# Feed-forward networks: x normed first from the third unit pair on, its two parts side by side in one moving operand of 512 columns

## The chip, the cores and the metric

The kernel runs on one core of one Trainium2 chip. The metric is the device time of one execution in microseconds (us), as the median of several runs.

## The reference, cut to what matters

One sequence of 256 tokens with 1024 channels goes through two small transformer stacks. Three of their stages are dense feed-forward networks, and only those are touched: one of the first stack (`ffn`), and two with a causal convolution of width 3 over the tokens in the second (`ffa`, `ffb`).

```
D_MODEL = 1024; SEQ = 256; D_FF = D_FF_2 = 2816

def rms_norm(x, g):
    y = x * rsqrt(mean(x * x, axis=-1) + EPS)
    return y * g

def swiglu(h, w_gate, w_up, w_down):                       # ffn
    return (silu(h @ w_gate) * (h @ w_up)) @ w_down

def conv_glu_ffn(h, w_in, conv_w, conv_b, w_out):          # ffa, ffb
    u = h @ w_in
    c = causal_conv(u, conv_w, width=3) + conv_b           # each channel by itself
    a, g = c[..., :D_FF_2], c[..., D_FF_2:]
    return (a * silu(g)) @ w_out

x = x + swiglu(rms_norm(x, ffn_norm[0]), ...)
h = h + conv_glu_ffn(rms_norm_2(h, norm_ffn[i]), ...)      # i = 0, 1
```

Around them stand a convolution stage, two attention stages, a mixture of experts and a pooling stage. All values are float32.

## The kernel before, in words

**Layout.** x stays in SBUF as `self.x`, channels on the 128 partitions: eight tiles of 128 channels, 256 tokens each. All weights come from DRAM as units of 128x2048 float32 (1 MB), in one fixed order, by the class `Stream`. TensorE multiplies in float32r. To keep float32 accuracy each operand is split into a high part (rounded to float32r) and a low part (the rest), and each product is made of three: high weights by high x, high weights by low x, low weights by high x (`mm3`, L468).

**The stream.** `load` (L304) sends SP's DMA for a unit into one of six `raw` buffers. `h` (L350) makes the high part `wh` on ScalarE (ACT, L359), `l` (L362) the low part `wl` on VectorE (DVE, L370) by subtraction. There are four `wh` and three `wl` buffers. `adv` (L380) goes to the next unit. So `h` works up to four units ahead of TensorE (PE) and `l` up to three. The order of the instructions on each engine is that of the code: nothing is reordered by a scheduler, and each engine takes its instructions in order.

**A feed-forward network (`ffn`, L918).** The 2816 inner channels are worked in 11 pairs of units, p = 0 to 10: the gate unit and the up unit of 256 inner channels. The order of the units is gate 0, up 0, gate 1, up 1, then gate p, up p, down p-2 for p = 2 to 10, and down 9 and down 10 at the end.

- Before it, `residual` (L627) adds the last stage to x, makes x times the norm's gain in two parts (`xh`, `xl`, L607 and L613) and sums the squares. The factor 1/rms of each token is not yet known then.
- `unit_B` (L473) multiplies one unit: for each of its two halves m of 128 inner channels and each of 8 channel tiles k three matmuls of 256 columns, 48 in all, into one PSUM bank with the two halves side by side.
- During pair 0 the sums of squares go through PE, and DVE makes 1/rms (L544 to L576). `bcast` brings it to all partitions as `rb` (L591, ACT).
- Since `xh` and `xl` lack 1/rms, the product is multiplied by `rb` as it leaves PSUM: one DVE operation of 512 columns, in `scaled` (L925, without convolution) or `convolved` (L936, with it, into the padded tile `cu`).
- `convolved` then makes tap 0 on ACT (L939) and taps 1 and 2 on DVE (L947, two operations of 256 columns each).
- `gate_out` adds Silu on ACT (L955). DVE multiplies up by gate (L973), ACT makes the high part of it (L975), DVE the low part (L982). These two halves are the moving operand of the down unit two pairs later (`unit_down`, L491, 48 matmuls of 256 columns).
- Calls of `st.h()` and `st.l()` stand between these steps, so the parts of later units are made on ACT and DVE between the steps of the current pair.

The PSUM banks of the gate and up units have the tag "g", of which there are four; the down units' sums have four more. Big SBUF tiles (`self.big`, 128x2048) come from a pool of six in turn.

Of the kernel before, what the change touches and what calls it, by code (L numbers as in the profile page):

```python
# [6 lines left out]
F32 = mybir.dt.float32  # L7
F32R = mybir.dt.float32r
I32 = mybir.dt.int32
AF = mybir.ActivationFunctionType  # L10
ALU = mybir.AluOpType
# [3 lines left out]
P = 128  # L15
S = 256
D = 1024
NT = D // P
# [57 lines left out]
def unit_plan():  # L76
# [8 lines left out]
    def ffn(ph, gate, up, g0, u0, down):  # L85
# [5 lines left out]
        for p in (NP_FF - 2, NP_FF - 1):  # L91
            u.append((ph, "row", down, 256 * p))

    ffn("ffn", "gate", "up", 0, 0, "down")
    for p in range(4):
        u.append(("att", "col", "w_kvf", 256 * p))
# [7 lines left out]
    for e in range(NE):  # L104
# [8 lines left out]
        u.append(("moe", "row", ("mdown", e), 2560))  # L113
    u.append(("pool", "pool", "pool", 0))
    ffn("ffa", "in0", "in0", FF, 0, "out0")
    u.append(("at2", "col", "qkv", 1024))
    for what in ATT2:
# [4 lines left out]
        elif what[0] == "o" and what[-1] != "+":  # L122
            u.append(("at2", "rowq", "o2", int(what[1])))
    ffn("ffb", "in1", "in1", FF, 0, "out1")
    return u

# [279 lines left out]
class Builder:  # L406
# [66 lines left out]
    def unit_B(self, tag, xs):  # L473
# [11 lines left out]
                    self.mm3(o, H[:, w], L[:, w], xs[0][:, a], xs[1][:, a], k == 0, k == NT - 1)  # L485
        return ps

    def acc_new(self):
        return [self.bank("acc") for _ in range(4)]

# [424 lines left out]
        return acc  # L915


    def ffn(self, xs, total, conv=None):  # L918
        nc, st = self.nc, self.st
        acc = None  # L920
        rb = None

        def scaled(ps, name):
            t = self.wk.tile([P, 512], F32, name=name)
            nc.vector.tensor_tensor(out=self.v2(t), in0=self.v2(ps), in1=self.rb2(rb), op=ALU.mult)  # L925
            st.h()
            st.l()
            return t

        def convolved(ps, tile0, name):  # L930

            W = S + 2
            up = self.wk.tile([P, 2 * W], F32, name="cu", tag="w1", bufs=4)
            u3 = up.rearrange("p (a w) -> p a w", a=2)
            nc.gpsimd.memset(u3[:, :, 0:2], 0.0)
            nc.vector.tensor_tensor(out=u3[:, :, 2:W], in0=self.v2(ps), in1=self.rb2(rb), op=ALU.mult)  # L936
            o = self.wk.tile([P, 512], F32, name=name)
            for m in range(2):
                nc.scalar.activation(out=o[:, m * S:(m + 1) * S], in_=up[:, m * W:m * W + S], func=AF.Identity,  # L939
                                     scale=self.c(f"fw{conv}", 3 * (tile0 + m), 1),  # L940
                                     bias=self.c(f"fb{conv}", tile0 + m, 1))
            st.h()
            st.l()
            for k in (1, 2):
                for m in range(2):
                    q = o[:, m * S:(m + 1) * S]
                    nc.vector.scalar_tensor_tensor(q, up[:, m * W + k:m * W + k + S],  # L947
                                                   self.c(f"fw{conv}", 3 * (tile0 + m) + k, 1), q,
                                                   op0=ALU.mult, op1=ALU.add)
            return o  # L950

        def gate_out(p, gps):
            t = scaled(gps, "gs") if conv is None else convolved(gps, 22 + 2 * p, "gs")
            sg = self.wk.tile([P, 512], F32, name="sg")
            nc.scalar.activation(out=sg, in_=t, func=AF.Silu)  # L955
            return sg

        pend = []
        for p in range(NP_FF):
            gps = self.unit_B("g", xs)  # L960
            st.adv()
            if p:
                sg = gate_out(p, gps)
                ups = self.unit_B("g", xs)
            else:
                r = self.stats(total)
                st.l()
                ups = self.unit_B("g", xs)
                rb = self.bcast(r)
                sg = gate_out(p, gps)  # L970
            st.adv()
            u = scaled(ups, "us") if conv is None else convolved(ups, 2 * p, "us")
            nc.vector.tensor_tensor(out=u, in0=u, in1=sg, op=ALU.mult)  # L973
            ah, al = self.parts()
            nc.scalar.activation(out=ah, in_=u, func=AF.Copy)  # L975
            if len(pend) == 2:
                if acc is None:
                    acc = self.acc_new()
                self.unit_down(acc, [pend.pop(0)], p == 2, False)
                st.adv()  # L980
                st.h()
            nc.vector.tensor_tensor(out=al, in0=u, in1=ah.bitcast(F32), op=ALU.subtract)  # L982
            st.l()
            pend.append((ah, al))
        self.unit_down(acc, pend, False, True)
        st.adv()
        st.adv()
        return acc
# [920 lines left out]
    def run(self):  # L1909
        st, ph = self.st, self.phases  # L1910
        st.h()
        st.l()
        st.h()
        upd = None
        if "conv" in ph:
            upd = self.added(self.conv(), "cbo")
        if "ffn" in ph:
            upd = self.added(self.ffn(*self.residual(upd, "gf0")))
        if "att" in ph:
            upd = self.added(self.att1(upd))  # L1920
        if "moe" in ph:
            upd = self.moe(upd)
        if "pool" in ph:
            upd = self.pool(upd)
        if "ffa" in ph:
            upd = self.added(self.ffn(*self.residual(upd, "hf0"), 0))
        if "at2" in ph:
            upd = self.added(self.att2(upd))
        if "ffb" in ph:
            upd = self.added(self.ffn(*self.residual(upd, "hf1"), 1))  # L1930
            self.final(upd)
            return
        if upd is not None:
            for b in range(4):
                upd(b)
        self.nc.sync.dma_start(out=self.A["out"], in_=self.x)
# [17 lines left out]
```

## Time and profile before

| | us |
|---|---|
| median of 3 runs | 1762.65 (1759.74 to 1765.97) |
| the profiled execution, its own time | 1759.57 |
| its span | 1757.8 |
| PE busy | 1705.6 (97% of the span) |
| PE weight loads busy | 1536.7 (87%) |
| DVE busy | 1394.4 (79%) |
| ACT busy | 1095.3 (62%) |

The page of a profile shows the busy time of each engine, the span in 40 slices, the DMA queues, the chain of work that ended last, and the costliest groups of instructions. Behind it stand other views of the same execution: the chain of waits in order of time, the timeline of one engine, and tables by stretches of time. Matmuls are pipelined, so the duration in a matmul's row is longer than the time from one start to the next. The pace of PE is read from the starts. The three networks lie at about 130 to 330 us (`ffn`), 1282 to 1473 us (`ffa`) and 1558 to 1749 us (`ffb`).

### The profile page before, as it was taken

What the parts mean: (1) busy time and instruction counts of PE and PEld (TensorE: products, weight loads), DVE (VectorE), ACT (ScalarE), POOL (GpSimd) and SP (SyncE); (2) the same over time, 40 slices, a digit from 0 to 9 for tenths busy, and PEclk for the clock granted to TensorE, in tenths of its full rate; (3) what the DMA queues carried; (4) which work ended last, traced back from release to release, by engine and by line L of the source; (5) the groups of instructions that cost most, each with busy time, mean ns of one, the idle gap of its engine ahead of it and who ended that gap; (6) DMA issues with size and microseconds to landing.
All of it is one profiled execution on the core that took longest, in us unless ns stands there. A gap on an engine that the chain in (4) does not pass through costs nothing. (4 is left out here: it accounts for less than half of the span.)

```text
span 1757.8 us, 26713 instructions
## 1 busy us (share of the span) xinstructions
PE 1705.6 (97%) x10780; PEld 1536.7 (87%) x10781; DVE 1394.4 (79%) x1649; ACT 1095.3 (62%) x1209; POOL 69.6 (4%) x114
## 2 busy tenths in 40 slices
PE   7979999999999999999999999999899999899998
PEld 6879999988888888888888888888789999899998
DVE  6976555765688988998998988988797777978766
ACT  4954443654587777777777777777555545756543
POOL 2800000010000000000000000000000000000000
PEclk9989999999999999999999999999999999999999
DMA  7235554443499799999999899999545554335440
GB/s 285 96 120 207 178 192 172 165 169 120 163 363 366 285 359 345 377 337 365 346 354 376 337 354 347 367 355 370 190 167 199 184 191 156 141 121 195 189 144 25
DMA packets 60560, 429.35 MB, mean 244 GB/s; under 512 B 6912, under 2 KB 6928, under 8 KB 9232
## 3 DMA queue, kind: packets, MB, share of 16 engines
q1 hardware_dynamic: 59760, 425.48, 64.8%
q0 software_dynamic: 672, 2.11, 0.4%
q8 instruction: 86, 1.41, 0.3%
q14 instruction: 42, 0.34, 0.1%
HBM read 426.50 MB, written 1.06 MB: 243 GB/s over the span
## 5 line engine op out<-in xcount | busy, mean ns | idle before, releaser
L370 DVE TENSOR_TENSOR wl<-raw,wh 128x2048 fp32r<-128x2048 f32 x384 | 870.2, 2286 | 41.0 <-PE ps_acc L466 20.4
L359 ACT ACTIVATE wh<-raw 128x2048 fp32r<-128x2048 f32 x384 | 734.0, 1915 | 243.3 <-PE ps_g L466 115.9
L466 PE MATMUL ps_g<-xh,wh 128*128 128x256 f32 x1136 | 322.7, 284 | 3.9 <-ACT xh L607 3.9
L466 PE MATMUL ps_g<-xl,wh 128*128 128x256 f32 x1136 | 323.4, 285 | 3.1 <-DVE xl L613 3.1
L466 PE MATMUL ps_g<-xh,wl 128*128 128x256 f32 x1136 | 321.9, 283 | 0.0
L466 PE MATMUL ps_g<-wh,xgh 128*128 128x512 f32 x704 | 276.5, 393 | 0.0
L466 PE MATMUL ps_g<-wh,xgl 128*128 128x512 f32 x704 | 274.3, 390 | 0.0
L466 PE MATMUL ps_g<-wl,xgh 128*128 128x512 f32 x704 | 274.2, 390 | 0.0
L466 PE MATMUL ps_acc<-parts,wh 128*128 128x256 f32 x1312 | 239.0, 284 | 0.7 <-DVE parts L511 0.5
L466 PE MATMUL ps_acc<-wh,parts 128*128 128x512 f32 x704 | 226.6, 392 | 4.2 <-ACT parts L510 4.2
L466 PEld LDWEIGHTS ps_g<-xl,wh 128*128 128x128 f32 x1136 | 218.4, 192 | 5.0 <-DVE xl L613 5.0
L466 PEld LDWEIGHTS ps_g<-xh,wh 128*128 128x128 f32 x1136 | 218.5, 192 | 4.2 <-ACT xh L607 4.1
L466 PEld LDWEIGHTS ps_g<-xh,wl 128*128 128x128 f32 x1136 | 218.5, 192 | 0.0
L466 PEld LDWEIGHTS ps_acc<-parts,wh 128*128 128x128 f32 x1312 | 204.7, 192 | 2.1 <-issue 0.9
L466 PE MATMUL ps_acc<-parts,wl 128*128 128x256 f32 x656 | 185.6, 283 | 0.0
L466 PEld LDWEIGHTS ps_acc<-wh,parts 128*128 128x128 f32 x704 | 131.4, 188 | 36.4 <-ACT parts L510 6.4
L466 PEld LDWEIGHTS ps_g<-wh,xgl 128*128 128x128 f32 x704 | 132.1, 188 | 28.1
L466 PEld LDWEIGHTS ps_g<-wh,xgh 128*128 128x128 f32 x704 | 132.3, 188 | 26.3
L466 PEld LDWEIGHTS ps_g<-wl,xgh 128*128 128x128 f32 x704 | 132.3, 188 | 26.2
L466 PE MATMUL ps_acc<-wl,parts 128*128 128x512 f32 x352 | 137.2, 390 | 0.7 <-DVE wl L370 0.7
L466 PEld LDWEIGHTS ps_acc<-parts,wl 128*128 128x128 f32 x656 | 125.9, 192 | 0.0
L511 DVE TENSOR_TENSOR parts<-ps_acc,parts 128x512 fp32r<-128x512 f32 (+1 forms) x48 | 31.0, 647 | 68.7 <-ACT parts L510 68.7
(309 smaller groups left out, 1970.1 us busy)
## 6 DMA issues: line engine op xcount, KB each, us to landing
raw<-ws SPq DMA_DIRECT2D x390, 1024.0 KB, 6.2
ahead<-ws SPq DMA_DIRECT2D x10, 1024.0 KB, 7.1
raw<-ws SPq DMA_DIRECT2D x4, 512.0 KB, 8.6
ck<-cdram POOLq DMA_DIRECT2D x8, 256.0 KB, 5.6
x<-xt SPq DMA_DIRECT2D x2, 512.0 KB, 4.2
out<-o SPq DMA_DIRECT2D x4, 256.0 KB, 2.3
cb<-cb SPq DMA_DIRECT2D x1, 617.5 KB, 15.5
raw<-band SPq DMA_DIRECT2D x1, 527.0 KB, 6.0
```

Source lines behind the costliest of these rows:

```text
L359: self.nc.scalar.activation(out=self.hi[i], in_=self.raw[i], func=AF.Copy)
L370: self.nc.vector.tensor_tensor(out=t, in0=raw, in1=self.hi[i].bitcast(F32), op=ALU.subtract)
L466: self.nc.tensor.matmul(out, lhsT, rhs, start=start, stop=stop, skip_group_check=True)
L511: self.nc.vector.tensor_tensor(out=l, in0=src, in1=h.bitcast(F32), op=ALU.subtract)
```

## The change

From pair 2 on, the gate and up units take a new moving operand, and their results leave PSUM in another way.

- Two new big tiles `ya` and `yb` hold x, normed with its gain and with `rb`, in two parts: for each channel tile k the 256 columns of the high part and, right beside them, the 256 of the low part. `normed(b)` makes two channel tiles of it: two DVE operations of 256 columns (x times gain times `rb`, into `xn`), one ACT copy of 512 columns (high part), one DVE subtraction of 512 columns (low part). `normed(0)` and `normed(1)` (into `ya`, k = 0 to 3) stand at the end of pair 0, `normed(2)` and `normed(3)` (into `yb`, k = 4 to 7) in pair 1, ahead of the step that takes the up product out of PSUM.
- `unit_W` multiplies a unit: for each half m and tile k one matmul of high weights by 512 columns (both parts), and one of low weights by the 256 columns of the high part. That is 32 matmuls in place of 48. Each half m has a PSUM bank of its own, in which the first 256 columns are a part of the sum and the other 256 the rest.
- `summed` takes a unit out of PSUM: for each half an ACT copy of the second 256 columns into SBUF and a DVE addition of the first 256. It takes the place of one DVE multiplication by `rb` of 512 columns.

Pairs 0 and 1 stay with `unit_B`, `xh`, `xl` and the multiplication by `rb`.

```diff
+    def unit_W(self, tag, ys):
+        H, L = self.st.cur()
+        pss = []
+        for m in range(2):
+            ps = self.bank(tag)
+            for k in range(NT):
+                w = slice(k * 256 + m * P, k * 256 + m * P + P)
+                y, o = ys[k // 4], (k % 4) * 512
+                self.mm(ps, H[:, w], y[:, o:o + 512], k == 0, False)
+                self.mm(ps[:, 0:S], L[:, w], y[:, o:o + S], False, k == NT - 1)
+            pss.append(ps)
+        return pss
...
-    def ffn(self, xs, total, conv=None):
+    def ffn(self, xs, total, gain, conv=None):
...
+        ys = [self.big(F32R, "ya"), self.big(F32R, "yb")]
+
+        def normed(b):
+            t = self.wk.tile([P, 512], F32, name="xn", tag="w1", bufs=4)
+            for m in range(2):
+                j = 2 * b + m
+                nc.vector.scalar_tensor_tensor(t[:, m * S:(m + 1) * S], self.x[:, j, :], self.c(gain, j, 1), rb,
+                                               op0=ALU.mult, op1=ALU.mult)
+            y = ys[b // 2][:, 1024 * (b % 2):1024 * (b % 2) + 1024].rearrange("p (a c s) -> p a c s", a=2, c=2)
+            nc.scalar.activation(out=y[:, :, 0, :], in_=self.v2(t), func=AF.Copy)
+            nc.vector.tensor_tensor(out=y[:, :, 1, :], in0=self.v2(t), in1=y[:, :, 0, :].bitcast(F32),
+                                    op=ALU.subtract)
+
+        def products(p):
+            return self.unit_W("g", ys) if p > 1 else self.unit_B("g", xs)
+
+        def summed(dst, ps, p):
+            if p < 2:
+                nc.vector.tensor_tensor(out=dst, in0=self.v2(ps), in1=self.rb2(rb), op=ALU.mult)
+                return
+            for m in range(2):
+                nc.scalar.activation(out=dst[:, m, :], in_=ps[m][:, S:2 * S], func=AF.Copy)
+                nc.vector.tensor_tensor(out=dst[:, m, :], in0=ps[m][:, 0:S], in1=dst[:, m, :], op=ALU.add)
...
-            nc.vector.tensor_tensor(out=u3[:, :, 2:W], in0=self.v2(ps), in1=self.rb2(rb), op=ALU.mult)
+            summed(u3[:, :, 2:W], ps, p)
...
             st.adv()
-            u = scaled(ups, "us") if conv is None else convolved(ups, 2 * p, "us")
+            if p == 1:
+                for b in (2, 3):
+                    normed(b)
+            u = scaled(ups, p, "us") if conv is None else convolved(ups, p, 2 * p, "us")
...
             nc.vector.tensor_tensor(out=al, in0=u, in1=ah.bitcast(F32), op=ALU.subtract)
+            if p == 0:
+                for b in (0, 1):
+                    normed(b)
             st.l()
```

The change moves instructions at these places. The rows are in the order in which the engine takes them.

DVE in `ffa`, from the end of pair 0 to the end of pair 1, before (`cu<-ps_g` is a product leaving PSUM, `wl` the low part of a later unit, `gs` and `us` the taps of gate and up):

```order
L982 TENSOR_TENSOR parts<-us,parts 128x512
L936 TENSOR_TENSOR cu<-ps_g,rb 128x2x256
L370 TENSOR_TENSOR wl<-raw,wh 128x2048
L947 SCALAR_TENSOR_TENSOR gs<-cu,cb,gs 128x256 x4
L936 TENSOR_TENSOR cu<-ps_g,rb 128x2x256
L370 TENSOR_TENSOR wl<-raw,wh 128x2048
L947 SCALAR_TENSOR_TENSOR us<-cu,cb,us 128x256 x4
```

The same stretch with the change:

```order
L1027 TENSOR_TENSOR parts<-us,parts 128x512
L946 SCALAR_TENSOR_TENSOR xn<-x,ca,rb 128x256 x2
L950 TENSOR_TENSOR ya<-xn,ya 128x2x256
L946 SCALAR_TENSOR_TENSOR xn<-x,ca,rb 128x256 x2
L950 TENSOR_TENSOR ya<-xn,ya 128x2x256
L959 TENSOR_TENSOR cu<-ps_g,rb 128x2x256
L370 TENSOR_TENSOR wl<-raw,wh 128x2048
L989 SCALAR_TENSOR_TENSOR gs<-cu,cb,gs 128x256 x4
L946 SCALAR_TENSOR_TENSOR xn<-x,ca,rb 128x256 x2
L950 TENSOR_TENSOR yb<-xn,yb 128x2x256
L946 SCALAR_TENSOR_TENSOR xn<-x,ca,rb 128x256 x2
L950 TENSOR_TENSOR yb<-xn,yb 128x2x256
```

The twelve new DVE operations of a network stand in two blocks, one ahead of gate 1's way out of PSUM, one behind gate 1's taps and ahead of up 1's way out.

PE at the start of gate 2 in the change (a wait for DVE is written behind the instruction that has it):

```order
L466 MATMUL ps_g<-xh,wl 128x256
L466 MATMUL ps_g<-ya,wh 128x512 [waits DVE_49]
L466 MATMUL ps_g<-ya,wl 128x256
L466 MATMUL ps_g<-ya,wh 128x512
L466 MATMUL ps_g<-ya,wl 128x256
L466 MATMUL ps_g<-ya,wh 128x512 [waits DVE_49]
L466 MATMUL ps_g<-ya,wl 128x256
L466 MATMUL ps_g<-ya,wh 128x512
L466 MATMUL ps_g<-ya,wl 128x256
L466 MATMUL ps_g<-yb,wh 128x512 [waits DVE_49]
L466 MATMUL ps_g<-yb,wl 128x256
```

Where every tile k had three matmuls of 256 columns there are now one of 512 and one of 256, and PE waits for DVE ahead of every second k, once for each `normed(b)`.

## Rows read from the trace of the kernel before

**Rows 1.** The page: busy time of each engine, share of the span, instructions.

```profile
PE 1705.6 (97%) x10780; PEld 1536.7 (87%) x10781; DVE 1394.4 (79%) x1649; ACT 1095.3 (62%) x1209; POOL 69.6 (4%) x114
```

**Rows 2.** Chain of waits, `ffa` and `ffb`: start us, us, what.

```profile
1282.92 33.45 PE ps_g L466 x277
1316.37 5.76 PE ps_acc L466 x48
1322.13 11.52 PE ps_g L466 x96
...
1443.09 11.54 PE ps_g L466 x96
...
1461.30 10.96 PE ps_acc L466 x89
...
1592.38 5.76 PE ps_acc L466 x48
```

**Rows 3.** Timeline of PE, mixture of experts: start us, us, engine, line, op, tiles.

```profile
704.34 0.39 PE L466 MATMUL ps_g<-wl,xgh 128*128 128x512 f32 x1
704.57 0.39 PE L466 MATMUL ps_g<-wh,xgl 128*128 128x512 f32 x1
...
706.84 0.39 PE L466 MATMUL ps_acc<-wh,parts 128*128 128x512 f32 x1
```

**Rows 4.** Timeline of DVE, `ffa`, pairs 0 and 1.

```profile
1301.42 0.69 DVE L973 TENSOR_TENSOR us<-us,sg 128x512 f32<-128x512 f32 x1
1302.81 0.69 DVE L982 TENSOR_TENSOR parts<-us,parts 128x512 fp32r<-128x512 f32 x1 [0.70 <-ACT parts L975]
1303.42 0.68 DVE L936 TENSOR_TENSOR cu<-ps_g,rb 128x512 f32<-128x512 f32 x1
1304.03 2.28 DVE L370 TENSOR_TENSOR wl<-raw,wh 128x2048 fp32r<-128x2048 f32 x1
1306.22 1.67 DVE L947 SCALAR_TENSOR_TENSOR gs<-cu,cb,gs 128x256 f32<-128x256 f32 x4
1307.81 0.69 DVE L936 TENSOR_TENSOR cu<-ps_g,rb 128x512 f32<-128x512 f32 x1
```

**Rows 5.** Timeline of ACT, `ffa`, pair 0.

```profile
1293.37 0.39 ACT L591 ACTIVATE rb<-ps_g 128x256 f32<-128x256 f32 x1 [7.60 <-PE ps_g L466]
...
1302.15 0.63 ACT L975 ACTIVATE parts<-us 128x512 fp32r<-128x512 f32 x1 [1.36 <-DVE us L973]
```

**Rows 6.** Timeline of DVE, `ffa`: operations of 256 columns, from SBUF and from PSUM.

```profile
1278.05 0.86 DVE L1791 SCALAR_TENSOR_TENSOR x<-ps_acc,cb,x 128x256 f32<-128x256 f32 x2
...
1282.40 0.87 DVE L613 SCALAR_TENSOR_TENSOR xl<-x,ca,xh 128x256 fp32r<-128x256 f32 x2
1283.19 1.14 DVE L535 TENSOR_TENSOR sq<-sq 128x512 f32<-128x512 f32 x2
```

**Rows 7.** Timeline of DVE, `ffb`, gate 1 leaves PSUM.

```profile
1579.82 0.68 DVE L936 TENSOR_TENSOR cu<-ps_g,rb 128x512 f32<-128x512 f32 x1
```

**Rows 8.** Timeline of DVE, `ffn`, pair 1.

```profile
148.00 0.68 DVE L925 TENSOR_TENSOR gs<-ps_g,rb 128x512 f32<-128x512 f32 x1
148.59 2.28 DVE L370 TENSOR_TENSOR wl<-raw,wh 128x2048 fp32r<-128x2048 f32 x1
153.03 0.69 DVE L925 TENSOR_TENSOR us<-ps_g,rb 128x512 f32<-128x512 f32 x1 [2.15 <-PE ps_g L466]
```

**Rows 9.** Stretches of 3 us: length, PE busy, granted clock, DMA share, GB/s.

```profile
462.00:465.00 3.00, 2.07 (x10) 0.50 0.09 36
465.00:468.00 3.00, 2.86 (x13) 0.50 0.00 0
...
1249.00:1252.00 3.00, 0.87 (x4) 1.00 0.06 19
1252.00:1255.00 3.00, 1.18 (x5) 0.80 0.15 22
1255.00:1258.00 3.00, 3.00 (x19) 0.63 0.80 330
1258.00:1261.00 3.00, 3.00 (x28) 1.00 0.01 3
```

**Rows 10.** Waits of DVE, 1283 to 1475 us: us in total, times, longest us.

```profile
DVE cu L936 <- PE ps_g L466: 29.8, 16, 2.7
```

More of the change, by code (lines that the diff above doesn't have):

```diff
@@ L921, in ffn, with scaled @@
         rb = None
-        def scaled(ps, name):
+        ys = [self.big(F32R, "ya"), self.big(F32R, "yb")]
[18 more added lines that the diff above has]
+                nc.vector.tensor_tensor(out=dst[:, m, :], in0=ps[m][:, 0:S], in1=dst[:, m, :], op=ALU.add)
+        def scaled(ps, p, name):
             t = self.wk.tile([P, 512], F32, name=name)
-            nc.vector.tensor_tensor(out=self.v2(t), in0=self.v2(ps), in1=self.rb2(rb), op=ALU.mult)
+            summed(self.v2(t), ps, p)
             st.h()
@@ L928, in scaled, with convolved @@
             return t
-        def convolved(ps, tile0, name):
+        def convolved(ps, p, tile0, name):
             W = S + 2
@@ L952, in gate_out @@
         def gate_out(p, gps):
-            t = scaled(gps, "gs") if conv is None else convolved(gps, 22 + 2 * p, "gs")
+            t = scaled(gps, p, "gs") if conv is None else convolved(gps, p, 22 + 2 * p, "gs")
             sg = self.wk.tile([P, 512], F32, name="sg")
@@ L959, in ffn @@
         for p in range(NP_FF):
-            gps = self.unit_B("g", xs)
+            gps = products(p)
             st.adv()
@@ L963, in ffn @@
                 sg = gate_out(p, gps)
-                ups = self.unit_B("g", xs)
+                ups = products(p)
             else:
@@ L967, in ffn @@
                 st.l()
-                ups = self.unit_B("g", xs)
+                ups = products(p)
                 rb = self.bcast(r)
@@ L1917, in run @@
         if "ffn" in ph:
-            upd = self.added(self.ffn(*self.residual(upd, "gf0")))
+            upd = self.added(self.ffn(*self.residual(upd, "gf0"), "gf0"))
         if "att" in ph:
@@ L1925, in run @@
         if "ffa" in ph:
-            upd = self.added(self.ffn(*self.residual(upd, "hf0"), 0))
+            upd = self.added(self.ffn(*self.residual(upd, "hf0"), "hf0", 0))
         if "at2" in ph:
@@ L1929, in run @@
         if "ffb" in ph:
-            upd = self.added(self.ffn(*self.residual(upd, "hf1"), 1))
+            upd = self.added(self.ffn(*self.residual(upd, "hf1"), "hf1", 1))
             self.final(upd)
```

## Prediction

> **What bounds the kernel now.** I read the page first: PE is busy for 97% of the span [rows 1], so time is won or lost where PE's stream is dense or broken. Then the chain of waits in the networks: in `ffa` it is PE alone from 1282.92 us to the end of the last up unit at 1454.63, in blocks of 5.76 us for 48 matmuls [rows 2]. That is 120 ns for each matmul of 256 columns, with no gap. A unit that is faster on PE therefore shortens a network one for one, and a stall of PE lengthens it one for one: nothing behind it has slack to give back. Last, the timelines of DVE and ACT around pairs 0 to 2, since the new operand is made there.
>
> The reader should see one thing in rows 4. Pair 1's gate product leaves PSUM on DVE at 1303.42, without a wait in its row, and the up product at 1307.81, again without one. Counted back from the down unit at 1316.37, up 2 runs from 1310.61, gate 2 from 1304.85, up 1 from 1299.09 [rows 2]. So gate 1 was done at 1299.09 and waited 4.3 us for DVE, and up 1 was done at 1304.85 and waited 3.0 us. DVE is behind in pairs 0 and 1, and later it waits for PE (29.8 us in 16 waits in `ffa`, [rows 10]). It costs nothing today, because only later units need what it makes. The change makes gate 2 need it at once.
>
> **The gain on PE.** In the mixture of experts eleven matmuls of 512 columns start between 704.34 and 706.84: 227 ns each [rows 3]. One of 512 and one of 256 columns take 227 + 120 = 347 ns, three of 256 take 360: 13 ns less. A unit has 16 such places: 0.21 us less (5.55 in place of 5.76). Nine pairs by two units by three networks are 54 units: 11.3 us. The rows' pace fits 13.3 ns for each matmul beside its columns (120 = 106.7 + 13.3 at 2.4 GHz, 227 = 213.3 + 13.3), and the change saves one such piece in three.
>
> The Trainium skill (TensorE: Matmul & The Clock Gate, section Back-to-back issue gap) gives a warm gap of N/2.4 + 2.5 ns. By that rule a place saves 2.5 ns and all 54 units 2.2 us. The rows of this kernel decide for 13.3.
>
> **The stall at gate 2.** A block `normed(b)` on DVE is two operations of 256 columns, a round trip to ACT, and one of 512 columns. The pair of L613 lasts 0.87 [rows 6]. From the end of DVE's L973 (1302.11) to the start of ACT's copy (1302.15) are 0.04, the copy takes 0.63, and DVE starts 0.03 later [rows 4, 5]. The subtraction lasts 0.69, and the next operation starts 0.61 after it. So a block takes 0.87 + 0.04 + 0.63 + 0.03 + 0.61 = 2.18 us of DVE's queue, and its part is ready 2.26 after its start. DVE takes its instructions in order, so it idles during the round trip. I take the rows as they are; without the round trip a block is 0.79 + 0.61 = 1.4, and with every operation 0.1 longer it is 2.6.
>
> In `ffa` the first block starts where L936 stood, at 1303.42. The parts for k = 0, 1 are ready at 1305.68, those for k = 2, 3 at 1307.86. Then come the old steps from L936 to the next L936 (1303.42 to 1307.81, 4.39 us, [rows 4]), and the third block starts at 1303.42 + 4.36 + 4.39 = 1312.17: k = 4, 5 ready at 1314.43, k = 6, 7 at 1316.61. PE could start gate 2 at 1304.85; two tiles k take it 0.69. It runs in four pieces at 1305.68, 1307.86, 1314.43 and 1316.61, then half m = 1 without a wait (2.78): the end is 1316.61 + 0.69 + 2.78 = 1320.08, where it was 1310.61. **9.5 us lost**, gate 2's own gain included.
>
> `ffb` has the same steps: the block starts at 1579.82 [rows 7], gate 2 could start at 1592.38 - 11.52 = 1580.86 [rows 2]. The last part is ready at 1593.01, gate 2 ends at 1596.48 in place of 1586.62: **9.9 lost**.
>
> `ffn` has no taps on DVE. The blocks start at 148.00 and up 1 ends at 153.00 [rows 8], so `ya` (152.44) is in time. Then gate 1's L925 (0.59) and a `wl` (2.20): the third block starts at 155.15, k = 4, 5 are ready at 157.41, k = 6, 7 at 159.59. PE reaches k = 4 at 154.39 and stands. Gate 2 ends at 163.06 in place of 158.76: **4.3 lost**.
>
> Together 23.7. The other 17 units of each network give back 51 x 0.21 = 10.7.
>
> **The clock.** The granted clock falls after PE has stood still. Between 1249 and 1255 PE was busy for 2.05 of 6 us, and the clock then read 0.80 and 0.63 and was full again at 1258 [rows 9]. With a lower level of half speed that is 0.4 x 3 + 0.74 x 3 = 3.4 us at half. In `ffa` and `ffb` PE would work 2.8 of some 12 us. I take one such 3.4 us each, in which PE would have done 1.7 us of work more: 3.4. At least nothing; at most twice that in each network (462 to 468 has 6 us at half, [rows 9]) and 1.7 in `ffn`: 8.5.
>
> **What hides, and the rest.** The way out of PSUM changes from one DVE operation (0.61 to the next) to two ACT copies (0.39 each by L591, [rows 5]) and two DVE additions (0.43 each by L1791, [rows 6]). A pair gains 4 x 0.43 - 2 x 0.61 = 0.5 us of DVE work and loses 0.4 of length; DVE's waits for PE, up to 2.7 us at one place, cover both [rows 10]. If that cover were gone, `wl` would be late next, and PE with it. At the end of `ffa` and `ffb` it is not hidden: after the last up unit (1454.63) PE waits for that product's parts, and the chain goes on at 1461.30 [rows 2], 6.67 later, while one down unit covers 5.76 and a few matmuls of the next the rest. There one half's copy and addition (0.39 + 0.07 + 0.43) take the place of 0.61: 0.3 each, 0.6 in all. ACT's copies queue behind its Silu and `wh`; ACT is busy 62% [rows 1], and `wh` is made a unit earlier than `wl`. A product now takes two of the four banks "g": gate 3 needs gate 2's, which are out a whole up and down unit earlier; up 2's second half needs up 1's, out by 1317.2, before gate 2's end. The two big tiles shift which buffer each later tile gets; their former owners are done by then, and SP's load of attention constants at the end of `ffa` falls on `xh`, last read in up 1. No DMA is added or moved past another; POOL's two small fills per pair stay where they are. All this at nothing.
>
> **Sum.** 23.7 - 10.7 + 3.4 + 0.6 = +17.0 us, against the profiled execution's own 1759.57: 1776.6. The median of the runs is 3.1 above that execution, which would make 1779.6. I say 1778. Bounds: with blocks of 1.4 the last parts come at 1313.5, 1589.9 and 156.5, the losses are 6.4, 6.8 and 1.2, and without clock and tail the sum is +4; with blocks of 2.6 the losses are 11.2, 11.6 and 6.0, and with 8.5 for the clock and 0.6 for the tail it is +27.
>
> **The rivals.**
> - *Forecast (0.62):* the stall outweighs the gain, one short fall of the clock.
> - *The clock stays low (0.17):* 8.5 in place of 3.4, so 1783. For it: gate 2 has four pieces with gaps between them. Against: after 1258 it was back at once.
> - *PE gets hardly faster (0.04):* if the 512 columns went at 237 to 240 ns beside a 256, 9 to 11.3 us of the gain are gone: 1787 to 1789. For it: no row before shows the two lengths in turn. Against: both lengths keep their pace over long runs [rows 2, 3]. The rule of the Trainium skill (same page and section) would give 1787; the rows so far don't bear it out.
> - *No stall, faster (0.08):* the parts are in time, and the kernel has its 11.3 less: 1750. It decides at k = 6 of gate 2: `normed(3)` must be ready by about 1307 in `ffa`. That holds if DVE isn't late there. For it: DVE has long waits in all later pairs. Against: rows 4 show none in pair 1, and DVE's order is fixed.
> - *They cancel (0.09):* blocks without the round trip and no fall of the clock: +4, 1764 to 1767. For it: ACT might find the copy's input earlier. Against: the same round trip stands in every pair, with 0.70 us of idle DVE [rows 4].
>
> **How the numbers follow.** About 0.3% (5.3 us) is what a measurement of this kernel can tell from no change. Slower: 0.62 + 0.17 + 0.04 = 0.83. Same 0.09, faster 0.08. The range leaves out the faster case, most of the cancelling one, and sums over +27: 1767 to 1790.
>
> **What would show it.** In the new trace, PE's waits in gate 2 for DVE's L950 should come to some 9.7 us in `ffa`, 10 in `ffb` and 4.5 in `ffn`; blocks from down 0 on should read 11.1 us for 64 matmuls of gate and up, in place of 11.52 for 96; the granted clock should dip once at each of the two long stalls. No waits for L950 would make the forecast wrong, a pair of gate and up at 11.5 or a stall at every pair would make it too small.

## The result, and the profile after

The change made the kernel slower: 1787.66 us (median of four executions, 1784.01 to 1796.61) against 1762.52 for the kernel before, measured beside it; ratio 1.0138 [1.0110, 1.0167]. The profiled execution took 1785.67 us, its span is 1783.9 (before 1757.8, so 26.1 more).

The rest of the kernel, whose code is the same in every run, varies from one execution to the next, with the granted clock in it: in the eleven profiled executions it took from 1188.7 to 1198.8 us. So I also compare the three networks alone. The length of a network is the time from DVE's first step of 1/rms (`v<-ps_g`) to the same step of the next stage, for `ffb` to its last addition onto x. "Down 0" is the time from the same mark to the start of the first down unit on PE.

| us | `ffn` | `ffa` | `ffb` | sum |
|---|---|---|---|---|
| length before | 191.54 | 191.87 | 185.18 | |
| length after | 196.81 | 202.29 | 196.12 | +26.6 |
| to down 0, before | 29.13 | 29.13 | 29.13 | |
| to down 0, after | 36.33 | 41.32 | 41.63 | +31.9 |
| so from down 0 to the end | -1.9 | -1.8 | -1.6 | -5.3 |

The whole loss lies ahead of down 0; behind it the wide operand does gain. The page after the change, and what PE waited for over the whole span (us in total, times, longest):

```profile
PE 1712.1 (96%) x9916; PEld 1498.8 (84%) x9917; DVE 1420.0 (80%) x1739; ACT 1140.1 (64%) x1329; POOL 69.6 (4%) x114
```

```profile
PE ps_g L466 <- DVE yb L950: 16.2, 6, 5.4
...
PE ps_g L466 <- DVE ya L950: 4.6, 4, 1.3
```

PE has 864 matmuls fewer than in [rows 1] and is busy 6.5 us longer: part of its work ran at a lower clock. The waits for L950 are all in gate 2. DVE's timeline in `ffa` with the change, where [rows 4] were:

```profile
1308.30 0.88 DVE L946 SCALAR_TENSOR_TENSOR xn<-x,ca,rb 128x256 f32<-128x256 f32 x2
1309.87 0.69 DVE L950 TENSOR_TENSOR ya<-xn,ya 128x512 fp32r<-128x512 f32 x1 [0.70 <-ACT ya L949]
1310.48 0.88 DVE L946 SCALAR_TENSOR_TENSOR xn<-x,ca,rb 128x256 f32<-128x256 f32 x2
1312.05 0.69 DVE L950 TENSOR_TENSOR ya<-xn,ya 128x512 fp32r<-128x512 f32 x1 [0.70 <-ACT ya L949]
1312.66 0.68 DVE L959 TENSOR_TENSOR cu<-ps_g,rb 128x512 f32<-128x512 f32 x1
...
1320.79 0.69 DVE L950 TENSOR_TENSOR yb<-xn,yb 128x512 fp32r<-128x512 f32 x1 [0.70 <-ACT yb L949]
```

Each block takes 2.18 us of DVE's queue (1308.30 to 1310.48), 0.70 of it idle. The last part is there at 1321.48, 13.18 after the first block began; the working gave 13.19. PE at the same place, four matmuls of gate 2 (in brackets the idle time ahead of one and what ended it):

```profile
1310.62 0.50 PE L466 MATMUL ps_g<-ya,wh 128*128 128x512 f32 x1 [0.89 <-DVE ya L950]
...
1312.80 0.51 PE L466 MATMUL ps_g<-ya,wh 128*128 128x512 f32 x1 [1.21 <-DVE ya L950]
...
1319.36 0.80 PE L466 MATMUL ps_g<-yb,wh 128*128 128x512 f32 x1 [5.39 <-DVE yb L950]
...
1321.54 0.80 PE L466 MATMUL ps_g<-yb,wh 128*128 128x512 f32 x1 [0.53 <-DVE yb L950]
```

These are the four pieces of the forecast. The chain of waits in `ffa` from there on, which answers to [rows 2]:

```profile
1321.54 11.90 PE ps_g L466 x52
1333.44 5.76 PE ps_acc L466 x48
1339.21 11.10 PE ps_g L466 x64
1350.31 5.75 PE ps_acc L466 x48
1356.06 11.31 PE ps_g L466 x64
...
1458.46 11.33 PE ps_g L466 x64
```

Two things differ from the forecast. The 52 matmuls behind the last part (two tiles k, half m = 1 and up 2) take 11.90, where the forecast's pace makes 0.69 + 2.78 + 5.55 = 9.02. And a pair of gate and up takes 11.10 only once; the other seven take 11.31. The first is the clock. Stretches of PE in `ffa`, then in `ffn` (length, PE busy, granted clock, DMA share, GB/s):

```profile
1306.00:1312.00 6.00, 4.70 (x36) 1.00 0.42 165
1312.00:1318.00 6.00, 1.17 (x4) 0.62 0.16 52
1318.00:1324.00 6.00, 4.11 (x11) 0.50 0.29 123
1324.00:1330.00 6.00, 6.00 (x28) 0.75 0.50 178
```

```profile
159.00:162.00 3.00, 1.79 (x8) 0.62 0.48 202
162.00:165.00 3.00, 3.00 (x11) 0.50 0.18 22
165.00:168.00 3.00, 3.00 (x15) 0.75 0.79 328
```

After PE stood, the clock is at 0.50, the lower of its two levels (1.2 GHz), and it stays there while PE works without a gap, in `ffn` too, where it waited only 4.3 us. What the low clock costs can be read from the starts on PE, one 512 and one 256 in turn:

```profile
1322.34 0.63 PE L466 MATMUL ps_g<-yb,wh 128*128 128x512 f32 x1
...
1322.98 0.63 PE L466 MATMUL ps_g<-ya,wh 128*128 128x512 f32 x1
```

That is 0.64 us in place of 0.35. Eight such places stand behind the last part (1321.54 to 1326.83): 8 x 0.29 = 2.3 of the 2.9 that the 52 matmuls take too long.

### The profile page after: what moved, and what is told of

Its sections match the earlier page's. It is cut to its first block, busy times and chain, and to the rows that moved or that the text cites. A ratio compares the mean times of both kernels' runs of the same rounds, so it can differ in the third digit from the quotient of the medians.

```text
span 1783.9 us, 25130 instructions
## 1 busy us (share of the span) xinstructions
PE 1712.1 (96%) x9916; PEld 1498.8 (84%) x9917; DVE 1420.0 (80%) x1739; ACT 1140.1 (64%) x1329; POOL 69.6 (4%) x114
## 5 line engine op out<-in xcount | busy, mean ns | idle before, releaser
L466 PE MATMUL ps_g<-yb,wh 128*128 128x512 f32 x432 | 163.1, 410 | 16.2 <-DVE yb L950 16.2
L466 PE MATMUL ps_g<-ya,wh 128*128 128x512 f32 x432 | 161.0, 406 | 4.6 <-DVE ya L950 4.6
L466 PEld LDWEIGHTS ps_g<-wl,xgh 128*128 128x128 f32 x704 | 132.3, 188 | 26.2
L466 PE MATMUL ps_g<-yb,wl 128*128 128x256 f32 x432 | 123.6, 286 | 0.0
L466 PE MATMUL ps_g<-ya,wl 128*128 128x256 f32 x432 | 123.2, 285 | 0.0
L466 PEld LDWEIGHTS ps_g<-yb,wh 128*128 128x128 f32 x432 | 83.7, 194 | 39.2 <-DVE yb L950 18.8
L466 PEld LDWEIGHTS ps_g<-ya,wh 128*128 128x128 f32 x432 | 82.9, 192 | 24.9 <-DVE ya L950 5.6
```

The costliest lines, as they stand in the source:

```text
L466: self.nc.tensor.matmul(out, lhsT, rhs, start=start, stop=stop, skip_group_check=True)
```

## The experiments

The theory after the result: (a) PE stands in gate 2 because DVE makes the parts late; (b) the low clock behind that wait costs more than I took; (c) the wide pairs are a little slower than the sum of their two paces, because the lengths take turns. Rivals: DVE's added work by itself holds PE up somewhere else; the wide pairs lose by themselves.

### The blocks alone, without the wide operand

All twelve DVE operations of a network stay, but every unit is multiplied as before.

```diff
-            return self.unit_W("g", ys) if p > 1 else self.unit_B("g", xs)
+            return self.unit_B("g", xs)
...
-            if p < 2:
+            if True:
```

> The four blocks stay on DVE and ACT where the change has them, but every unit is multiplied as before (unit_B) and leaves PSUM as before; ya and yb are made and never read. Theory (the loss is PE's wait for these parts, DVE's lateness by itself is hidden): span within 2 us of before, 1758 to 1760, no PE wait on DVE in pairs 1 to 3, clock full. Rival (some 8.7 us of DVE work in pairs 0 and 1 hold PE up in any case, over PSUM banks or late low parts wl): 8 us or more in each of ffa and ffb, span 1775 or more, with PE waits on wl or on the way out of PSUM.

Measured: 1772.24 us (one execution). Against the kernel before, the lengths of `ffn`, `ffa` and `ffb` ("networks", from here on) are +0.0, +5.8, +6.2. That is not the 2 us or less that the theory gave. PE no longer waits for L950, but for the next thing in DVE's queue. PE's waits over the span, DVE and PE in the chain at down 0 of `ffa`, and the stretches there:

```profile
PE ps_acc L466 <- DVE wl L370: 6.2, 3, 2.7
```

```profile
1316.87 2.21 DVE wl L370
...
1319.12 8.42 PE ps_acc L466 x46
```

```profile
1317.00:1320.00 3.00, 0.88 (x4) 0.72 0.00 0
1320.00:1323.00 3.00, 3.00 (x16) 0.50 0.84 306
1323.00:1326.00 3.00, 3.00 (x19) 0.64 0.13 52
```

Down 0's `wl` stands behind the last block and is late, and then the clock falls: 46 matmuls take 8.42 where 48 take 5.76 [rows 2]. So in `ffa` and `ffb` the blocks cost some 6 us even if gate 2 does not need them: to that extent the rival of DVE's added work is right. In the change this is covered by the longer wait in gate 2, and nothing is lost behind down 0. In `ffn`, which has no taps on DVE, the blocks cost nothing.

### The 512s of a half first, then its 256s

Within each half m the eight matmuls of 512 columns come first and the eight of 256 after them, in place of taking turns.

```diff
             for k in range(NT):
...
                 self.mm(ps, H[:, w], y[:, o:o + 512], k == 0, False)
+            for k in range(NT):
+                w = slice(k * 256 + m * P, k * 256 + m * P + P)
+                y, o = ys[k // 4], (k % 4) * 512
                 self.mm(ps[:, 0:S], L[:, w], y[:, o:o + S], False, k == NT - 1)
```

> The change, but within each half m the eight matmuls of 512 columns come first and the eight of 256 after them, in place of taking turns. In the changed kernel a pair of gate and up takes 11.31 us from pair 4 on and 11.10 in a few pairs before. Theory (taking turns between the two lengths costs some 6 ns for each pair of matmuls; alone they keep 227 and 120): every wide pair 11.1 us, some 4.5 to 5 us less than the change over all three networks. Rival (the loss lies in the 512 columns of high and low part themselves or in the two banks, not in the turns): 11.31 as before, no change of the span beyond 1.5 us. In both, the stall at gate 2 stays.

Measured: 1787.89 us (one execution), networks +26.2. The chain of waits in `ffa`, gate 2 on, and PE's waits over the span:

```profile
1323.89 12.76 PE ps_g L466 x58
...
1342.41 11.17 PE ps_g L466 x64
```

```profile
PE ps_g L466 <- DVE yb L953: 18.6, 6, 5.8
```

A pair takes 11.17 in place of 11.31, so two thirds of the difference to 11.10 are the taking of turns; the last third stays open. That is worth 2.8 us behind down 0. The total gains nothing by it, where 4.5 to 5 were expected: gate 2's first 512s need all parts at once, less work stands ahead of the late ones (58 matmuls behind the last part, not 52), and the wait for `yb` is 2.4 longer.

### Extra matmuls in gate 2's waits

```diff
+                if fill is not None and m == 0:
+                    for i in range(fill[2].get(k, 0)):
+                        self.mm(fill[0], H[:, 0:P], fill[1][0][:, 0:512], i == 0, i == fill[2][k] - 1)
...
+                n = {4: 12, 6: 5} if conv is None else {0: 4, 2: 5, 4: 23, 6: 2}
+                return self.unit_W("g", ys, (self.bank("acc"), xs, n))
```

> The change, with additional matmuls of 512 columns into an unused bank at gate 2 where PE stands still (before k = 0, 2, 4, 6: 4, 5, 23, 2 in ffa and ffb; 12 and 5 before k = 4 and 6 in ffn), results not used. They are to fill the wait, about as long as it is. Theory (after the stall PE runs gate 2 and up 2 at half clock, which cost 2.7 us in each network by the changed kernel's trace): granted clock stays 1.00 from pair 1 to 3, the span is 7 to 8 us shorter than the change's (1783.9), near 1776. Rival (the half clock falls together with the wait and costs nothing): the span stays within 2 us or grows by the added work.

Measured: 1779.81 us (one execution), networks +2.7, +8.0, +8.4, together 19.0: 7.6 less than with the change, though PE does 85 matmuls more and DVE is as late as it was. The same stretches of `ffa`:

```profile
1306.00:1312.00 6.00, 5.93 (x33) 1.00 0.14 55
1312.00:1318.00 6.00, 5.64 (x26) 1.00 0.49 175
1318.00:1324.00 6.00, 5.27 (x29) 1.00 0.10 15
1324.00:1330.00 6.00, 6.00 (x39) 1.00 0.48 171
```

The clock stays at 1.00, and the 52 matmuls behind the last part take 9.45 in place of 11.90. The low clock costs 2.5 us in each of the three networks, near the 2.3 read from the starts on PE. This settles (b).

### Wide only from pair 6 on, the blocks at the ends of pairs 1 to 4

```diff
-            return self.unit_W("g", ys) if p > 1 else self.unit_B("g", xs)
+            return self.unit_W("g", ys) if p > 5 else self.unit_B("g", xs)
...
+            if 1 <= p <= 4:
+                normed(p - 1)
```

> The four blocks are spread over the ends of pairs 1 to 4 (one each, behind the low part of the next unit), and the wide units begin with pair 6: 30 units in place of 54, everything else of them as in the change. Theory (the whole loss is the stall at the first wide unit and the clock behind it; each wide unit gains 0.1 us at 11.31 a pair): no PE wait on ya or yb, clock full, 30 x 0.1 = 3 us less, 0.6 us more at the two ends, so 2 to 3 us below before, ratio 0.998 to 0.999. Rival (the wide units or their way out of PSUM cost by themselves): 30 of 54 parts of the loss, some 14 us above before, ratio 1.008.

Measured: 1758.37 us (median of ten) against 1762.79; ratio 0.9972 [0.9954, 0.9989]; networks -1.07, -0.91, -0.90. The last narrow pair and the first wide one in `ffa`'s chain:

```profile
1357.25 11.52 PE ps_g L466 x96
1368.77 5.76 PE ps_acc L466 x48
1374.53 11.31 PE ps_g L466 x64
```

No wait for L950 is left and there is a gain, of 0.21 for each of five pairs. So the wide pairs do not lose by themselves, and the DVE work of the twelve operations is hidden at this place in its queue. With PE's waits for L950 in the change this settles (a). The rival of the wide pairs falls. The rival of DVE's added work holds only as the first experiment shows it: at the old place the blocks would cost some 6 us in `ffa` and `ffb` at down 0 if gate 2 did not wait for them first.

### All four blocks at the end of pair 0

```diff
-            if p == 1:
-                for b in (2, 3):
-                    normed(b)
...
-                for b in (0, 1):
+                for b in range(4):
```

> The change with all four blocks at the end of pair 0, ahead of gate 1's way out of PSUM. Nothing else is moved. Theory (gate 2 ends when the last part is ready plus 0.69 + 2.78 us): the last part comes one way out of PSUM, one low part wl and in ffa and ffb four taps earlier (4.4 us, in ffn 2.8), so PE's waits for ya and yb fall by 11 to 12 us from 20.8 in all, and with less time at half clock the span is some 12 to 15 us below the change's 1783.9: 1769 to 1772. Rival (what holds is DVE's backlog as a whole, e.g. wl of down 0, as in the run with the blocks alone): the wait moves to down 0 or up 2 and the span stays above 1778.

Measured: 1774.74 us (one execution), networks -0.1, +5.4, +6.0: together 11.3, 15.3 less than with the change; expected were 12 to 15. PE's waits over the span:

```profile
PE ps_g L466 <- DVE yb L950: 5.0, 6, 1.2
PE ps_g L466 <- DVE ya L950: 4.6, 4, 1.3
```

The waits fall from 20.8 to 9.6. The 11.2 between are DVE's old steps that stood between the second and the third block: 4.39 us each in `ffa` and `ffb` [rows 4], 2.8 in `ffn`, 11.6 in all. Of the other 4 of the 15.3 the clock in `ffn` explains some 2.6, as it cost there: PE was now busy for 4.51 of 6 us (156 to 162 us), and the clock stayed at 1.00. In `ffa` and `ffb` it still fell to 0.50 (1315 to 1318 and 1599 to 1602 us).

### Wide from pair 6 on, with the 512s first

The edit is that of the fourth and of the second experiment together.

> The run with the blocks at the ends of pairs 1 to 4 and wide units from pair 6, now with the eight matmuls of 512 columns of a half ahead of its eight of 256. Theory (turns between lengths cost about 6 ns each): wide pairs 11.17 us in place of 11.31, 15 pairs, 2 us less than with turns; and the ACT copy can start before the half is done, 0.3 us less at each end. Ratio to before 0.996 to 0.997, span near 1755. Rival (with the stall gone the order makes no difference): 11.31 a pair, ratio 0.998.

Measured: networks -1.74, -1.58, -1.57, together 2.0 less than in the fourth experiment, as expected for 0.14 x 5 pairs x 3. The 0.3 us less at each end, expected too, did not come: the gain is 0.67 in every network and the five pairs make all of it. The time does not show the gain either: 1763.05 us (median of ten) against 1762.92, ratio 0.9988 [0.9967, 1.0008]. Its executions lie from 1754.7 to 1766.2, those of the kernel before from 1759.5 to 1766.6. How much of that spread belongs to other stages was not settled; for the total this run is inconclusive.

### The parts made in fewer DVE steps, x times `rb` on POOL

x times `rb` is made for all four pairs of tiles by POOL; ACT makes the high part with the gain as its scale; DVE makes the low part in one operation of 256 columns for each tile. The 512s come first everywhere but in the first halves of pair 2's two units.

```diff
+                nc.gpsimd.tensor_tensor(out=self.v2(t), in0=self.x[:, 2 * b:2 * b + 2, :], in1=self.rb2(rb),
+                                       op=ALU.mult)
...
+                nc.scalar.activation(out=y_of(b, m)[:, 0:S], in_=xns[b][:, m * S:(m + 1) * S], func=AF.Copy,
+                                     scale=self.c(gain, 2 * b + m, 1))
...
+                nc.vector.scalar_tensor_tensor(y[:, S:2 * S], xns[b][:, m * S:(m + 1) * S], self.c(gain, 2 * b + m, 1),
+                                               y[:, 0:S].bitcast(F32), op0=ALU.mult, op1=ALU.subtract)
```

> Wide units from pair 2 as in the change, but the parts are made with less work on DVE: GpSimd multiplies x by rb (four operations of 512 columns in pair 0), ACT makes the high part with the gain as its scale (8 of 256), DVE only the low part (8 of 256, 3.2 us, all at the end of pair 0, no round trips). Half m = 0 of gate 2 takes turns between the lengths, all other halves have the 512s first. Theory (the loss is DVE's lateness at gate 2 and at down 0; 3.2 us of DVE in place of 8.7 fits before both): PE waits at gate 2 of at most 2 us in ffa and ffb, none in ffn, clock full; 27 pairs gain 0.35 us = 9.4, so span 1750 to 1753, ratio 0.995 to 0.997. Rival (GpSimd's 7 us beside DVE slow DVE down, or ACT's eight copies make the taps late): waits of 4 us and more and a fall of the clock, span 1760 or more.

Measured: 1767.75 us (median of ten) against 1762.92, ratio 1.0025 [1.0005, 1.0046]; networks -3.1, +2.4, +2.8. `ffn` does what it should; `ffa` and `ffb` miss, with waits in gate 2 of 3.5 and 3.9 us where at most 2 were expected. The timelines of POOL, ACT and DVE in `ffa`, pair 0:

```profile
1295.88 5.06 POOL L953 TENSOR_TENSOR xb<-x,rb 128x512 f32<-128x512 f32 x4 [19.18 <-DVE wl L370]
1300.87 0.21 POOL L996 MEMSET cu<- 128x4 f32 x4
```

```profile
1301.02 1.09 ACT L1000 ACTIVATE gs<-cu,cb 128x256 f32<-128x256 f32 x2 [5.21 <-POOL cu L996]
```

```profile
1301.65 1.77 DVE L1008 SCALAR_TENSOR_TENSOR gs<-cu,cb,gs 128x256 f32<-128x256 f32 x4 [5.13 <-ACT gs L1000]
```

POOL's four products (5.06 us) stand ahead of the small fill that the taps' tile `cu` needs. So tap 0 of gate 0 waited on ACT (5.21 us), DVE stood idle for 5.13 us behind it, and all that follows was late again. That is another cause than the rival named (POOL slowing DVE, or ACT's copies).

### The same with x times `rb` on DVE

```diff
-                nc.gpsimd.tensor_tensor(out=self.v2(t), in0=self.x[:, 2 * b:2 * b + 2, :], in1=self.rb2(rb),
+                nc.vector.tensor_tensor(out=self.v2(t), in0=self.x[:, 2 * b:2 * b + 2, :], in1=self.rb2(rb),
```

> The same with the product of x and rb on DVE (4 operations of 512 columns behind gate 0's taps) in place of GpSimd: 5.6 us of DVE in place of 3.2. Theory: the last low part in ffa is ready near 1309 on the clock of before, gate 2 ends some 2 us late in each of ffa and ffb, down 0 is just in time: span 2 to 4 us above the run with GpSimd, 1753 to 1757. Rival (GpSimd beside DVE is the dearer way): below it.

Measured: 1764.34 us (one execution), networks -3.08, -0.87, -0.81. One wait of 1.50 us is left at gate 2 of `ffa`:

```profile
1311.67 0.50 PE L466 MATMUL ps_g<-ya,wh 128*128 128x512 f32 x1 [1.50 <-DVE ya L969]
```

PE's granted clock is 1.00 through it. In `ffn` no wait for the parts is left: nine pairs at 0.35 less give the 3.1. Over the networks this run is 6.9 us shorter than the one with POOL, and not 2 to 4 longer as expected: that was the rival's forecast. Its total does not show this, since the rest of the kernel took 1198.8 us in this one execution, 1189.2 before.

### The version that is faster than both

As the one before, but in `ffa` and `ffb` wide from pair 3 on, with the parts of two blocks made in pair 0 and two in pair 1.

```diff
+        first = 2 if conv is None else 3
...
-            return self.unit_W("g", ys, p == 2) if p > 1 else self.unit_B("g", xs)
+            return self.unit_W("g", ys, p == first) if p >= first else self.unit_B("g", xs)
...
+            if p < (1 if conv is None else 2):
+                for b in range(4) if conv is None else (2 * p, 2 * p + 1):
+                    y_low(b)
```

> The parts made as in the run with the product of x and rb on DVE, wide units from pair 2 in ffn and from pair 3 in ffa and ffb, there with the low parts two at the end of pair 0 and two at the end of pair 1; the 512s of a half ahead of its 256s but for the first half of the first wide unit. Theory (no part is late any more, each wide pair gains 0.35 us, and the end of a network loses nothing): no PE wait on ya or yb or on wl of down 0, clock full through pairs 1 to 4, ffn 3.1 us shorter as in the run before, ffa and ffb 8 x 0.35 = 2.8 to 3 each; 9 us in all, ratio 0.994 to 0.996. Rival (DVE's 5.6 us more in pairs 0 and 1 still reach PE in ffa and ffb, at down 0): waits on wl there, ffa and ffb no shorter than before, ratio 0.998 or more.

Measured: 1755.80 us (median of twelve) against 1766.04, ratio 0.9954 [0.9936, 0.9971]; networks -3.1, -1.9, -1.8. In `ffa`, the first wide pair (up to its end) and the second in the chain of waits, and PE's one wait there for DVE:

```profile
1318.53 11.22 PE ps_g L466 x63
1329.74 5.76 PE ps_acc L466 x48
1335.50 11.17 PE ps_g L466 x64
```

```profile
1317.71 0.39 PE L466 MATMUL ps_g<-ya,wh 128*128 128x512 f32 x1
1318.53 0.38 PE L466 MATMUL ps_g<-ya,wl 128*128 128x256 f32 x1 [0.43 <-DVE wl L370]
```

There are no waits for the parts. The sum is -6.9, not the -9 that I expected: eight wide pairs at 0.35 less would be 2.8 in `ffa` and in `ffb`, and about 0.9 of that is not there. Most of it is in the first wide pair: by the starts on PE it takes 11.87 us in `ffa` (1317.71 to 1329.58) and 11.95 in `ffb`, where the later ones take 11.17. In `ffa` its second matmul starts 0.82 after its first, where one of 512 columns takes 0.23: `wl` is late. The rest, some 0.15 in each, is at the end of the network, behind the last up unit.

## Why the prediction was right, and where it was not

Direction and mechanism held, and the time lies in the range; but the loss is 26, where the sum said 17.0. That the range holds is in part luck: its upper end was made of blocks of 2.6 us, which did not come, and had no room for the slower pace, which did. Measured against the networks' marks:

- **The stall** is as worked out. The block is 2.18 us, the last part comes 13.18 after the first block began. The waits in gate 2 are 8.0 us in `ffa`, 8.5 in `ffb` and 4.3 in `ffn` where 9.7, 10 and 4.5 were named, as some of the work between the pieces ran slower instead. In `ffa` the last of the four pieces starts 11.97 after up 1's end, and the working gave 1316.61 - 1304.85 = 11.76. Up to down 0 the stall without the clock should cost 9.3, 9.7 and 4.1 (up 2's gain taken off), and the measured 12.2, 12.5 and 7.2 exceed these by 2.9, 2.8 and 3.1.
- **The clock** is the first mis-sized term: "one such 3.4 us each ... 3.4", and nothing for `ffn`. The run with extra matmuls puts it at 7.6 in all, about 2.5 in each of the three networks. It fell in all three, not only at the two long stalls. (The 2.9, 2.8 and 3.1 by the marks, together 8.8, hold more than the clock: the last piece starts 0.2 later than worked out in `ffa`, and with the clock full the 52 matmuls still take 9.45, not 9.02.) I had priced a short fall after [rows 9] and none after a wait of 4.3. The upper bound, on which the rival with a clock that stays low rests (8.5), came nearer to the total, though with too much in `ffa` and `ffb` and too little in `ffn`.
- **The pace** is the second: "227 + 120 = 347 ns". In turn the two take 353 in seven of the eight pairs from down 0 on, so a pair is 11.31, not 11.10. Behind down 0 the gain is 5.3 where 9.5 was worked out. The rival of a hardly faster PE was right in kind and too large: 6 ns of the 13 are gone, not 10 to 13. The Trainium skill (TensorE: Matmul & The Clock Gate, section Back-to-back issue gap) has 2.5 ns a place, for an isolated matmul and not for a stream with weight loads; the prediction left that limit out. It does not fit either: measured are 360 - 353 = 7 ns in turn, and 360 - 349 = 11 with the 512s first (11.17 us for 32 places).
- **The tail** was put 0.3 longer in `ffa` and `ffb`, and grew by half of that: PE goes on 6.81 us after the last up unit (1469.79 to 1476.60 in `ffa`), where it was 6.67.
- **"All this at nothing"** holds for the change as it stands. The sentence on `wl`, which would be late next if DVE's cover were gone, was meant for the later pairs. The first experiment shows it in pair 2: without gate 2's wait, down 0's `wl` is up to 2.7 us late and costs 6 us in `ffa` and in `ffb`. DVE's backlog there was a second limit that the forecast did not price.

Together: 17.0 + 5.4 up to down 0 (8.8 - 3.4; 4.2 of it is the clock, 7.6 - 3.4) + 4.2 behind it (9.5 - 5.3: the pace, less the shorter tail) = 26.6. The sum must come out, since its parts are read off the networks' marks; what stands apart from them is the clock's 7.6, and the pace of 353 ns read from the chain.

## What to carry to other kernels

An operand that a matmul needs at once has to be priced by the queue of the engine that makes it, as it stands at that place: DVE, busy for 79% of the span, was 12 us late here, and the same twelve operations cost nothing some pairs later. Where PE is the bound, a stall of some us has to be counted with the slow stretch behind it, here another 2.5 us each. And a new mix of matmul lengths has to be timed as it is issued, not by the sum of the two paces.

## What the runs showed of the hardware that was not expected

- PE worked on at 0.50 for some 5 us after it had its last data: in `ffa` the windows read 0.62, 0.50 and 0.75 from 1312 to 1330, and the starts keep the slow pace from 1321.54 to 1326.83. At 0.50 one 512 and one 256 take 0.64 us, less than twice the 0.35 of full clock. A wait of 1.50 us ahead of a dense stretch left the clock at 1.00; a stretch with 0.88 of 3 us busy (the first experiment) was followed by 0.50. Extra matmuls with unused results in the waits paid for themselves: the networks were 7.6 us shorter by them.
- One 512 and one 256 in turn have two paces: 347 ns in pair 3 of `ffn` and `ffa` (the 11.10 in the chain above), 353 in all other pairs of the change from pair 3 on (11.31 and 11.33). With the extra matmuls pair 3 has 347 in all three networks, with all four blocks in pair 0 in none. Nothing in between was seen, and why it is the one or the other is open. With the 512s of a half first it is 349 for both together (11.17).
